# A mixture-of-experts layer: the experts' down product in three float32r passes, the routing weight folded into gate times up, g_ffn moved to the sums, and a scatter that skips empty places

## The chip, the cores and the metric

The program runs on one core of a Trainium2 chip. The metric is the device time of one execution in microseconds; the kernel before is given as the median of three runs.

## What is computed

Two transformer blocks run one after the other on 512 tokens of width 1024, in float32. The change lies in the mixture-of-experts part of the first block. Each token goes to 8 of 64 experts; its expert outputs are weighted, summed, multiplied by the row `g_ffn` and added to `x`.

```python
def swiglu(x, wg, wu, wd):
    return (jax.nn.silu(x @ wg) * (x @ wu)) @ wd
...
def moe_ffn(h, ...):
    scores = sigmoid(h @ w_router)
    _, idx = lax.top_k(scores + b_router, TOP_K)          # 8 of 64
    wts = (chosen scores / their sum * ROUTE_SCALE)
    ...
    def expert_block(acc, blk):                            # up to 128 rows of one expert
        tok, wt, e = blk
        yb = swiglu(h_pad[tok], w_e_gate[e], w_e_up[e], w_e_down[e]) * wt[:, None]
        return acc.at[tok].add(yb), None
    ...
    return swiglu(h, w_sh_gate, w_sh_up, w_sh_down) + routed[:n]
...
    y = moe_ffn(h2, ...)
    return x + g_ffn * y.reshape(b, s, d)
```

An expert's gate and up weights are 1024x256 each, its down weights 256x1024: 3 MB in all.

## The kernel before

The program goes through the first block's attention and gating (to about 600 us), the router, the experts (about 620 to 1358 us), a short turn to the second block (to about 1395 us), and the second block with its own large products. `moe` (L763) runs the experts.

**One expert** is `expert_block` (L1040). 128 places hold the expert's tokens; a place without a token is empty. The tokens' rows `xg` were gathered from DRAM (`expert_rows`, indices `gidx`). TensorE transposes them (`p_xt`, 8 transposes) and `split` (L104) cuts the result into a float32r high part (ScalarE, L105) and a low part (VectorE, L106): `xt`. The gate and up weights come as two 1 MB loads (`raw`), are split in four pieces of 128x1024 into `whi` and `wlo` (the pool `pair`, three buffers each), and each piece serves 6 products of `mm` (L91: high by high, high by low, low by high, all float32r): 24 matmuls of 512 columns into `p_gu`. ScalarE takes Silu of the gate half (L1060), VectorE multiplies by the up half (L1061): `ea`. Two transposes (`p_at`, L1064) and a copy by VectorE (L1066) make `eat`.

**The down product** is in plain float32 (L1072): four matmuls, from `eat` and the third `raw` buffer as it was loaded, into two banks `p_y`. In the profile each float32 matmul shows as two instructions. VectorE then reads each bank and multiplies by the place's routing weight `wsl` and by `grow`, which is `g_ffn` laid over all partitions (L1075): `ey`. A DMA issued by GpSimd scatters the 128 rows of `ey` and adds them in DRAM into `yd` (L1076). The two tensors `yd` have 640 rows: an empty place p has the index 512 + p, so its row is added into a spare row that nobody reads. The gather takes the same indices with a bound of 511, and skips them. Successive experts alternate between the two `yd`; the last two share one.

64 experts and one spare block (`spare`, L1088, for tokens beyond 128) make 65 such blocks; the loop `overflow` runs no further block here. Beside them run the shared expert's products (`p_sh`, L983 and L1011), the lists of places (`slots`), and transposes of `x`.

**What sets the order.** Over most of the experts' part a scheduler of the framework sets each engine's order at build time; each engine then works its list strictly in that order. Waits are semaphores. The loads go through SP's queue into nine `raw` buffers in turn: six of the pool `raw2` (`RAW2`, L31) and three of `raw`. The first six loads are issued during the product before (L668).

**The turn** to the second block: `routed_first` (L1135) loads the first `yd` (two tiles `raw`), `routed_second` (L1144) adds it to `x`; the second `yd` is loaded as four tiles `yx` (L1210) after the last scatter has landed, and `routed` adds each (L1217), multiplies by the norm's row (L1218) and sums squares, tile by tile. TensorE's next products (`p_xh`, L1237) wait for that.

## Time and profile before

| | |
|---|---|
| Runs of the kernel before (us) | 3177.44, 3180.88, 3176.13; median 3177.44 |
| The profiled execution (us) | 3173.92, its span 3172.1 |
| Experts' part, from its first `p_y` to its last | 635.8 to 1357.2 us |
| Engines over the whole span | TensorE 97% busy, VectorE 71%, ScalarE 44%, GpSimd 18% |
| DMA over the whole span | 251 GB/s mean |

An engine's busy share is an average over stages with different limits, so the experts' part is read by itself: how much of it each engine works, what ended each engine's waits, and what the DMA queues carried. "PE" is TensorE, "PEld" its weight loads, "DVE" VectorE, "ACT" ScalarE, "POOL" GpSimd, "SPq" the queue of loads.

### The profile page before, as it was taken

The numbers are of one execution on the slowest core, as the hardware profiler recorded it, in microseconds if no ns is written. First come the engines' busy times: TensorE is split into PE (matmuls) and PEld (weight loads), VectorE is DVE, ScalarE is ACT, GpSimd is POOL, SyncE is SP. The second block draws the span as 40 slices with busy tenths as digits, with TensorE's granted clock in tenths as the row PEclk, the third lists the DMA queues.
The fourth block names the chain that finished last, engine by engine and source line by source line (L and its number), as shares of the span: only waits on it lengthen the run. The fifth ranks groups of instructions, "written<-read, shape, count | busy, mean of one in ns | idle before, by whom it ended". The sixth has DMA issues, their size and how long they took to land.

```text
span 3172.1 us, 43671 instructions
## 1 busy us (share of the span) xinstructions
PE 3062.8 (97%) x16232; PEld 2479.5 (78%) x16232; DVE 2238.7 (71%) x4079; ACT 1383.4 (44%) x2199; POOL 578.9 (18%) x448
## 2 busy tenths in 40 slices
PE   8999999999999999969999999999999999999999
PEld 4777888666666766657777788899999998888887
DVE  7467654587777777756633334899998887888887
ACT  5257423454444544434445324544444443333332
POOL 0200000122222222200000000033333233222221
PEclk9999999899999999989999999999999999999999
DMA  7554545399999999952121122487789989999997
GB/s 248 175 159 145 220 158 203 125 359 338 335 344 334 358 349 346 317 170 83 41 85 62 70 93 95 139 283 268 278 312 348 332 332 344 349 348 354 353 339 270
DMA packets 237626, 782.01 MB, mean 247 GB/s; under 512 B 28884, under 2 KB 110292, under 8 KB 191588
## 3 DMA queue, kind: packets, MB, share of 16 engines
q1 hardware_dynamic: 169072, 574.02, 49.0%
q0 software_dynamic: 65424, 198.81, 20.2%
q10 hardware_dynamic: 2916, 6.37, 0.6%
q8 instruction: 128, 2.10, 0.3%
q14 instruction: 86, 0.70, 0.1%
HBM read 694.38 MB, written 101.97 MB: 251 GB/s over the span
## 4 chain that ended last, share of the span: by engine, by line
PE 49%; DVE 6%; issue 1%; ACT 1%; DMA 1%; ACTq 0%; DVEq 0%; POOL 0%; POOLq 0%
PE p_y L102 16%; PE p_pu L102 12%; PE p_za L102 3%; PE p_z L102 2%; PE p_all L1267 2%; PE p_rg L102 1%; DVE wlo L106 1%; PE p_pq L102 1%; PE p_mx L102 1%; PE p_yr L102 1%; DVE prow L2010 1%; PE r_s L1614 1%; PE r_y L1624 1%; PE p_ya L102 1%; PE p_gt L1979 1%
## 5 line engine op out<-in xcount | busy, mean ns | idle before, releaser
L105 ACT ACTIVATE whi<-raw 128x1024 fp32r<-128x1024 f32 (+1 forms) x686 | 711.5, 1049 | 1135.4 <-PE p_pu L102 259.7
L106 DVE TENSOR_TENSOR wlo<-raw,whi 128x1024 fp32r<-128x1024 f32 (+1 forms) x686 | 822.6, 1207 | 350.2 <-ACT whi L105 338.9
L102 PE MATMUL p_pu<-xp,whi 128*128 128x384 f32 x2048 | 531.3, 338 | 5.0 <-ACT pact L1845 4.8
L102 PEld LDWEIGHTS p_pu<-xp,whi 128*128 128x128 f32 x2048 | 369.2, 188 | 7.9 <-ACT pact L1845 7.6
L102 PE MATMUL p_gu<-whi,xt 128*128 128x512 f32 x1040 | 356.8, 411 | 0.2 <-ACT whi L105 0.2
L102 PE MATMUL p_pu<-xp,wlo 128*128 128x384 f32 x1024 | 344.8, 338 | 4.7 <-DVE wlo L106 4.7
L102 PE MATMUL p_y<-whi,vhi 128*128 128x512 f32 x768 | 299.1, 389 | 3.0 <-ACT vhi L2060 1.6
L102 PE MATMUL p_y<-wlo,vhi 128*128 128x512 f32 x768 | 298.9, 389 | 0.0
L2000 POOL DMA_INDIRECT prow<-in_pu_rows,rows x128 | 198.0, 1547 | 513.9 <-DVE prow L2010 365.6
L1072 PE MATMUL p_y<-raw,eat 128*128 128x512 f32 x520 | 237.1, 597 | 2.7 <-DVE eat L1066 1.5
L102 PE MATMUL p_y<-whi,vlo 128*128 128x512 f32 x768 | 237.8, 389 | 0.0
L102 PEld LDWEIGHTS p_gu<-whi,xt 128*128 128x128 f32 x1040 | 197.4, 190 | 50.4 <-issue 11.2
L102 PE MATMUL p_gu<-wlo,xt 128*128 128x512 f32 x520 | 223.0, 429 | 4.9 <-DVE wlo L106 4.7
L2000 POOL DMA_INDIRECT prow<-in_pv_rows,rows x128 | 139.5, 1090 | 363.0 <-DVE yr L2016 349.7
L102 PEld LDWEIGHTS p_pu<-xp,wlo 128*128 128x128 f32 x1024 | 192.3, 188 | 10.4 <-DVE wlo L106 10.2
L1072 PEld LDWEIGHTS p_y<-raw,eat 128*128 128x128 f32 x520 | 97.7, 191 | 101.6 <-issue 89.5
L102 PEld LDWEIGHTS p_y<-whi,vhi 128*128 128x128 f32 x768 | 144.1, 188 | 33.5 <-ACT vhi L2060 2.0
L1076 POOL DMA_INDIRECT yd<-ey,gidx x64 | 117.5, 1836 | 285.1 <-DVE ey L1075 268.1
L102 PEld LDWEIGHTS p_y<-wlo,vhi 128*128 128x128 f32 x768 | 144.2, 188 | 30.0
L102 PEld LDWEIGHTS p_y<-whi,vlo 128*128 128x128 f32 x768 | 144.2, 188 | 29.9
L2016 DVE SCALAR_TENSOR_TENSOR yr<-prow,pdots,yr 128x1024 f32<-128x1024 f32 x128 | 163.8, 1280 | 0.2
L2010 DVE SCALAR_TENSOR_TENSOR prow<-prow,xr 128x1024 f32<-128x1024 f32 x128 | 155.5, 1219 | 3.1 <-DMA prow<-in_pu_rows,rows 3.0
(703 smaller groups left out, 5558.7 us busy)
## 6 DMA issues: line engine op xcount, KB each, us to landing
raw<-in_w_moe SPq DMA_DIRECT2D x195, 1024.0 KB
raw<-in_pu SPq DMA_DIRECT2D x64, 1024.0 KB
raw<-in_pv_rows SPq DMA_DIRECT2D x64, 1024.0 KB
raw<-in_w_mod SPq DMA_DIRECT2D x24, 1024.0 KB
gd<-gst SPq DMA_DIRECT2D x12, 2048.0 KB
vgt<-gd SPq DMA_DIRECT2D x32, 768.0 KB
actd<-pact SPq DMA_DIRECT2D x54, 384.0 KB
vact<-actd SPq DMA_DIRECT2D x54, 384.0 KB
```

What stands on the lines that cost most here:

```text
L102: nc.tensor.matmul(out, a, b, start=start and i == 0, stop=stop and i == len(passes) - 1)
L105: self.nc.scalar.activation(hi, src, AF.Copy)
L106: (lo_engine or self.nc.vector).tensor_tensor(lo, src, hi.bitcast(F32), ALU.subtract)
L1072: nc.tensor.matmul(py, at[:, 128 * k:128 * k + 128], wd[:, 1024 * k + 512 * n:1024 * k + 512 * n + 512], start=k == 0, stop=k == 1)
L1076: nc.gpsimd.indirect_dma_start(out=yd[:], out_offset=bass.IndirectOffsetOnAxis(ap=gi, axis=0), in_=y[:], in_offset=None, bounds_check=639, ...
L1267: self.nc.tensor.matmul(pts[i][:, :264], w[a][:, 128 * k:128 * k + 128], self.hn[b][:, k, 264 * i:264 * i + 264], start=k == 0 and n == 0, ...
L1614: nc.tensor.matmul(pt[:m, :n], self.rk[r:r + 64, g, 128 * kt:128 * kt + m], self.rq[r:r + 64, g, 512 - n:], start=True, stop=True)
L1624: nc.tensor.matmul(o, sts[kt][:, 128 * (i - kt):128 * (i - kt) + 128], v[:, 128 * kt:128 * kt + 128], start=False, stop=kt == i)
L1979: nc.tensor.matmul(pt[:, i, :], hots["hot2"][:, g, :, t], hots["ghi"][:, g, :, t], start=True, stop=False)
L2000: nc.gpsimd.indirect_dma_start(out=t[:], out_offset=None, in_=A["pu_rows" if i < 128 else "pv_rows"], in_offset=bass.IndirectOffsetOnAxis( ...
L2010: nc.vector.scalar_tensor_tensor(t, t, 1.0, self.xr, ALU.mult, ALU.mult, accum_out=dots[:, k:k + 1])
L2016: nc.vector.scalar_tensor_tensor(self.yr, t, dots[:, k:k + 1], self.yr, ALU.mult, ALU.add)
```

## The change

1. The down product goes through `mm` in three float32r passes. `eat` becomes a high and a low tile (`split` of `p_at`), and the down weights are split in two pieces of 128x1024 into `dhi` and `dlo`, two buffers each, in the pool of the experts' small tiles. Both banks `p_y` are filled together, the first half of the weights for both and then the second.
2. The routing weight is multiplied in with gate times up (L1061). `ey` is then a plain copy out of `p_y`, by ScalarE.
3. `g_ffn` is multiplied into the sums, once for each of the two `yd` after they are loaded (in `routed_second` and in `routed`). `grow` moves to a pool that lives that long.
4. The scatter's bound is 511, so that it skips empty places, and `yd` has 512 rows.
5. `RAW2` is 4: seven `raw` buffers in turn, and the last two of the first six loads are issued by GpSimd, in `moe`, behind the first two gathers.

```diff
-RAW2 = 6
+RAW2 = 4
...
-            self.yd = [d.tile([640, 1024], F32, name=f"yd{i}") for i in range(2)]
+            self.yd = [d.tile([512, 1024], F32, name=f"yd{i}") for i in range(2)]
...
-                            for i in range(5):
+                            for i in range(4):
                                 nc.gpsimd.dma_start(y[128 * i:128 * i + 128, :], self.macc)
...
-        nc.vector.tensor_mul(a, a, pg[:, 256:])
+        nc.vector.scalar_tensor_tensor(a, a, ws, pg[:, 256:], ALU.mult, ALU.mult)
...
-        at = ms.tile([128, 256], F32, name="eat", tag="eat")
-        nc.vector.tensor_copy(at, pt[:, :256])
+        at = [ms.tile([128, 256], F32R, name=f"eat{i}", tag=f"eat{i}") for i in range(2)]
+        self.split(*at, pt[:, :256])
         y = ms.tile([128, 1024], F32, name="ey", tag="ey")
         wd = part(2)
+        py = [ps.tile([128, 512], F32, name="p_y", tag="y") for n in range(2)]
+        for k in range(2):
+            hi, lo = (ms.tile([128, 1024], F32R, name=n, tag=n) for n in ("dhi", "dlo"))
+            self.split(hi, lo, wd[:, 1024 * k:1024 * k + 1024])
+            for n in range(2):
+                self.mm(py[n], tuple(t[:, 128 * k:128 * k + 128] for t in at), (hi[:, 512 * n:512 * n + 512], lo[:, 512 * n:512 * n + 512]),
+                        k == 0, k == 1)
         for n in range(2):
-            py = ps.tile([128, 512], F32, name="p_y", tag="y")
-            for k in range(2):
-                nc.tensor.matmul(py, at[:, 128 * k:128 * k + 128], wd[:, 1024 * k + 512 * n:1024 * k + 512 * n + 512],
-                                 start=k == 0, stop=k == 1)
-            o = slice(512 * n, 512 * n + 512)
-            nc.vector.scalar_tensor_tensor(y[:, o], py, ws, self.grow[:, o], ALU.mult, ALU.mult)
+            nc.scalar.activation(y[:, 512 * n:512 * n + 512], py[n], AF.Copy)
         nc.gpsimd.indirect_dma_start(out=yd[:], out_offset=bass.IndirectOffsetOnAxis(ap=gi, axis=0),
-                                     in_=y[:], in_offset=None, bounds_check=639, oob_is_err=True, compute_op=ALU.add)
+                                     in_=y[:], in_offset=None, bounds_check=511, oob_is_err=False, compute_op=ALU.add)
...
         for x, y in zip(self.xr, self.y0):
+            self.nc.vector.tensor_mul(y, y, self.grow[:, None, :].to_broadcast([128, 2, 1024]))
             self.nc.vector.tensor_add(x, x, y)
...
+            nc.vector.tensor_mul(ys[t], ys[t], self.grow)
             nc.vector.tensor_add(x[t], x[t], ys[t])
```

The scheduler orders the experts' part anew. TensorE, about expert 30, before: transposes of a later expert's rows (`p_xt`), of this one's `ea` (`p_at`), products of the next expert (`p_gu`), and the down product in one piece.

```order
L1046 MATMUL p_xt<-ident,xg_5302 128x128 x8
L102 MATMUL p_gu<-whi,xt_9501 128x512
L1064 MATMUL p_at<-ident,ea 128x128 x2
L102 MATMUL p_gu<-wlo,xt_9501 128x512
L102 MATMUL p_gu<-whi,xt_9502 128x512
L102 MATMUL p_gu<-whi,xt_9501 128x512
L102 MATMUL p_gu<-wlo,xt_9501 128x512
L102 MATMUL p_gu<-whi,xt_9502 128x512
L102 MATMUL p_gu<-whi,xt_9501 128x512
L1072 MATMUL p_y<-raw,eat 128x512 x4
```

After, at a like place; of the two tiles `eat` the first (9041) is the high part and the second (9042) the low one.

```order
L102 MATMUL p_y<-dhi,eat_9041 128x512
L102 MATMUL p_y<-dlo,eat_9041 128x512
L102 MATMUL p_y<-dhi,eat_9041 128x512
L102 MATMUL p_y<-dlo,eat_9041 128x512
L102 MATMUL p_gu<-wlo,xt_9091 128x512
L102 MATMUL p_gu<-whi,xt_9092 128x512
L102 MATMUL p_gu<-whi,xt_9091 128x512
L102 MATMUL p_gu<-wlo,xt_9091 128x512
L102 MATMUL p_gu<-whi,xt_9092 128x512
L102 MATMUL p_gu<-whi,xt_9091 128x512
L102 MATMUL p_y<-dhi,eat_9042 128x512 x2
L102 MATMUL p_y<-dhi,eat_9041 128x512
```

The down product now stands in two parts with six products of another expert between them: the four matmuls that need only the high part of `eat` come first.

ScalarE, about the same experts, before: the splits of the weights and rows and Silu, the same sequence for each expert.

```order
L105 ACTIVATE whi<-raw 128x1024 x4
L105 ACTIVATE xt_7036<-p_xt 128x512 x2
L1060 ACTIVATE ea<-p_gu 128x256
L105 ACTIVATE whi<-raw 128x1024 x4
L105 ACTIVATE xt_7178<-p_xt 128x512 x2
L1060 ACTIVATE ea<-p_gu 128x256
```

After, for somewhat over two experts:

```order
L105 ACTIVATE dhi<-raw 128x1024 x2
L105 ACTIVATE eat_7991<-p_at 128x256
L1077 ACTIVATE ey<-p_y 128x512 x2
L105 ACTIVATE whi<-raw 128x1024 x3
L105 ACTIVATE dhi<-raw 128x1024 x2
L105 ACTIVATE whi<-raw 128x1024 x2
L1077 ACTIVATE ey<-p_y 128x512 x2
L105 ACTIVATE whi<-raw 128x1024
L105 ACTIVATE xt_8240<-p_xt 128x512 x2
L1060 ACTIVATE ea<-p_gu 128x256
L105 ACTIVATE whi<-raw 128x1024 x2
L105 ACTIVATE eat_8095<-p_at 128x256
```

Each expert has five more instructions on ScalarE, and the copies `ey`, which wait for the end of a down product, stand ahead of the next splits of weights.

VectorE in the turn, before: two tiles `yx` with what follows them.

```order
L1217 TENSOR_TENSOR h2f_4832<-h2f_4832,yx 128x1024
L1218 TENSOR_TENSOR x<-h2f_4832,gf 128x1024
L1221 TENSOR_SCALAR xst<-xst 128x1
L1217 TENSOR_TENSOR h2f_4832<-h2f_4832,yx 128x1024
L1218 TENSOR_TENSOR x<-h2f_4832,gf 128x1024
```

After:

```order
L1220 TENSOR_TENSOR yx<-yx,grow 128x1024
L1221 TENSOR_TENSOR h2f_4830<-h2f_4830,yx 128x1024
L1222 TENSOR_TENSOR x<-h2f_4830,gf 128x1024
L1225 TENSOR_SCALAR xst<-xst 128x1
L1220 TENSOR_TENSOR yx<-yx,grow 128x1024
L1221 TENSOR_TENSOR h2f_4830<-h2f_4830,yx 128x1024
L1222 TENSOR_TENSOR x<-h2f_4830,gf 128x1024
```

One multiplication stands ahead of each addition.

## Rows read from the trace of the kernel before

**Rows 1.** The page: each engine's busy time and share over the span.
```profile
PE 3062.8 (97%) x16232; PEld 2479.5 (78%) x16232; DVE 2238.7 (71%) x4079; ACT 1383.4 (44%) x2199; POOL 578.9 (18%) x448
```

**Rows 2.** Busy time by stretch: one slice of the experts' part, the whole part, three later stretches.
```profile
core 0: us, PE busy (x) PEld busy (x) DVE busy (x) ACT busy (x) POOL busy (x), PEclk, DMA share, GB/s
1100.00:1150.00 50.00, 47.72 (x200) 31.16 (x200) 36.07 (x57) 19.13 (x26) 12.46 (x9) 0.93 1.02 352
640.00:1357.00 717.00, 705.55 (x3020) 478.38 (x3019) 538.89 (x787) 345.20 (x461) 195.05 (x123) 0.99 0.98 339
2110.00:2300.00 190.00, 181.93 (x1017) 175.09 (x1017) 185.83 (x668) 86.86 (x123) 71.68 (x43) 1.00 0.77 274
2300.00:2400.00 100.00, 97.66 (x700) 92.95 (x699) 93.15 (x140) 44.21 (x73) 37.19 (x23) 1.00 0.89 324
2400.00:2600.00 200.00, 200.00 (x1483) 194.97 (x1482) 177.01 (x256) 88.92 (x145) 60.47 (x43) 1.00 0.91 335
```

**Rows 3.** Waits in the experts' part: waiter, what ended it, us, times, longest.
```profile
ACT whi L105 <- PE p_gu L102: 235.8, 113, 10.2
...
PE p_gu L102 <- DVE wlo L106: 4.7, 5, 1.6
```

**Rows 4.** Waits of SP's queue from 600 to 1400 us.
```profile
SPq L1027 <- DVE wlo L106: 318.4, 85, 15.7
SPq L1027 <- PE p_y L1072: 178.4, 51, 12.5
```

**Rows 5.** Timeline of TensorE: one down product and the next instruction; start, us, what.
```profile
1323.89 3.60 PE L1072 MATMUL p_y<-raw,eat 128*128 128x512 f32 x8
1327.33 0.60 PE L1046 MATMUL p_xt<-ident,xg 128*128 128x128 f32 x4
```

**Rows 6.** The chain in a later stage: 48 float32r matmuls of 512 columns in a row.
```profile
1812.59 11.14 PE p_za L102 x48
```

**Rows 7.** Groups of the experts' part by shape: count | busy, mean ns | idle before.
```profile
L106 DVE TENSOR_TENSOR wlo<-raw,whi 128x1024 fp32r<-128x1024 f32 x249 | 299.4, 1221 | 89.1 <-ACT whi L105 87.9
L105 ACT ACTIVATE whi<-raw 128x1024 fp32r<-128x1024 f32 x249 | 257.8, 1064 | 243.2 <-PE p_gu L102 235.8 <-PE p_at L1064 4.1 <-DVE ea L1061 0.9
...
L1075 DVE SCALAR_TENSOR_TENSOR ey<-p_y,wsl,grow 128x512 f32<-128x512 f32 x125 | 89.1, 745 | 12.4 <-PE p_y L1072 12.1
...
L105 ACT ACTIVATE xt<-p_xt 128x512 fp32r<-128x512 f32 x123 | 67.7, 595 | 72.6 <-PE p_gu L102 65.8 <-PE p_xt L1046 5.4
...
L1060 ACT ACTIVATE ea<-p_gu 128x256 f32<-128x256 f32 x63 | 24.6, 390 | 25.9 <-PE p_gu L102 25.9
```

**Rows 8.** DMA queues and indirect issues from 700 to 1300 us.
```profile
q1 hardware_dynamic: 23470, 165.89, 69.1%
q0 software_dynamic: 14813, 40.39, 29.7%
...
xg<-h2d,gidx POOLq DMA_INDIRECT x51
yd<-ey,gidx POOLq DMA_INDIRECT x50
```

**Rows 9.** The chain through the turn: start, us, what.
```profile
1354.00 1.54 DMA yd<-ey,gidx
...
1363.76 10.65 DMA yd<-ey,gidx
```

**Rows 10.** Timeline of the turn: start, us, engine, line, what.
```profile
1363.23 2.29 DVE L1146 TENSOR_TENSOR h2f<-h2f,raw 128x2048 f32<-128x2048 f32 x1 [4.63 <-DMA raw<-yd]
...
1379.10 1.22 DVE L1217 TENSOR_TENSOR h2f<-h2f,yx 128x1024 f32<-128x1024 f32 x1
...
1380.35 1.23 DVE L1218 TENSOR_TENSOR x<-h2f,gf 128x1024 f32<-128x1024 f32 x1
```

**Rows 11.** Timeline of the start: the first gather on GpSimd and two splits.
```profile
613.71 1.11 POOL L1031 DMA_INDIRECT xg<-h2d,gidx  x1 [14.09 <-DVE ov_t L1119]
...
629.92 2.00 ACT L105 ACTIVATE whi<-raw 128x1024 fp32r<-128x1024 f32 x2
```

More of the change, by code (lines that the diff above doesn't have):

```diff
@@ L716, in ffn_begin @@
         self.r4 = r.tile([128, 4], F32, name="r4")
+        self.grow = r.tile([128, 1024], F32, name="grow")
         r = self.pool(self.rs, "h2r", side="right")
@@ L771, in moe @@
             self.sact = q.tile([128, 2, 512], F32, name="sact")
-            self.grow = q.tile([128, 1024], F32, name="grow")
             self.xr = [t.rearrange("p a b -> p (a b)").rearrange("p (t d) -> p t d", d=1024) for t in self.h2f]
```

## The prediction

> **What bounds the kernel now.** I read the busy times by stretch first, then who waits for whom in the experts' part, then the sizes of single instructions there. Over the span TensorE is busy 97% [rows 1], but that is a mean over stages. In the experts' part, 640 to 1357 us, it is busy 705.55 of 717 us, at 0.99 of its clock, while VectorE has 538.89 (75%) and ScalarE 345.20 (48%); the DMA share is 0.98 [rows 2]. Two readings compete: TensorE or the transfers. The waits decide for TensorE: ScalarE waits 235.8 us for `p_gu` to give split buffers back, so it stands ahead of TensorE, and TensorE's largest wait for a split is 4.7 us [rows 3]. SP's queue waits for buffers to come free (318.4 and 178.4 us) [rows 4]; no compute engine has a load among its long waits. So the transfers keep up, with little to spare, and the time of this part is TensorE's work plus what it stands idle: 11.5 us, 1.6%. There are 65 expert blocks, and the window of 717 us holds 717 / 11.27 = 63.6 of them (721.4 us from the first `p_y` to the last, 64 steps).
>
> **TensorE's part of the change.** Before, the down product is 8 instructions: from 1323.89 to the next at 1327.33, 3.44 us, 0.430 each [rows 5]. A float32r matmul of 512 columns takes 11.14 / 48 = 0.232 us in a row of 48 [rows 6]. After, there are 2 halves x 2 banks x 3 passes = 12 of them: 2.79 us. That is 0.65 us less in each block, 65 x 0.65 = **-42 us**. All of it is on the path as long as TensorE is the bound.
>
> The Trainium skill, "FP8 and Floating Point Precision", section "TensorE Precision Notes", says that true FP32 takes four passes through the array, of which the change would drop one: 4 x 0.232 x 65 = 60 us by that rule, an estimate. The trace differs: it shows two instructions of 0.430 for a float32 matmul, 0.86 and not 4 x 0.232 = 0.93, and the measured one is used.
>
> **VectorE.** Each block gains two `dlo` of the shape of `wlo`, 299.4 / 249 = 1.20 us, and loses two `ey`, 89.1 / 125 = 0.71 [rows 7]: +0.98. The low part of `eat` takes the place of a copy of its size, and gate times up stays one instruction: 0. Over 63.6 blocks 538.89 + 62 = 601 us, now in 717 - 41 = 676 us: 89%.
>
> **ScalarE.** Each block gains two `dhi` like `whi`, 257.8 / 249 = 1.04, two `ey` out of a bank like `xt`, 67.7 / 123 = 0.55, and the high part of `eat`, about one Silu, 24.6 / 63 = 0.39 [rows 7]: +3.55. 345 + 226 = 571 of 676 us: 85%.
>
> **What the fuller engines cost TensorE.** Each works its list in order, so a matmul can now wait for a split that stands behind something else; before, this hardly occurred. No row of this part shows it; three later stretches do, where TensorE also lives on splits [rows 2]: VectorE at 88.5% leaves TensorE idle 0 of 200 us, at 93% 2.3%, at 98% 4.2%. With 89%, VectorE would be next to the first of them. But ScalarE is at 44 to 46% there and at 85% here, and its new copies `ey` wait for the end of a down product ahead of the next weights; the low `eat` needs ScalarE and then VectorE, one hand-over more than now. So I take the worst of the three, 4.2% of 676 = 28 us instead of 11.5: **+17 us**. Ends: 0, and twice that idle share (57 us, +45). Own buffers for `dhi` and `dlo` keep the splits of the down weights from taking the three pairs that feed `p_gu`; without them this term would be the main one.
>
> **The transfers.** 128 rows of 4 KB are 0.524 MB a scatter; 50 of them are 26.2 of the 40.39 MB of the software queue, and the 51 gathers have 14.2, 0.28 MB or some 68 rows each [rows 8]. So a gather, with a bound of 511, does leave out empty places, and the scatter will. 512 tokens x 8 fill 4096 of 65 x 128 = 8320 places; 65 rows less in each block. The queue holds the 16 engines 29.7% of 600 us for some 51 blocks, 3.5 us a block for about 196 rows; by rows that frees 1.2 us, more if an adding row costs more than a plain one. TensorE's new pace is 11.27 - 0.65 = 10.6 us and the transfers need 11.27 x 0.98 - 1.2 = 9.9 (93%): they stay hidden, for 0. If rows were not skipped, 11.0 us of transfers would be the new pace and eat the gain; that is a rival below. Two `raw` buffers less leave seven, over two blocks ahead of TensorE; and a down buffer is free after its split and not after its matmuls. 0, at most one late load of 3 us now and then, which is in the upper end.
>
> **The start.** The two loads that GpSimd now issues stand behind the first gathers, at 613.71 and just after [rows 11], and hold its next gathers back by their issue only. A load of 1 MB takes 3 us at the part's 339 GB/s [rows 2]; their data, expert 1's second half and down weights, are wanted near 630, when the splits of that time run [rows 11]. 0; if late, 3 to 4 us.
>
> **The turn.** Four multiplications of 128x1024 stand ahead of four additions of 1.22 us on VectorE, which works there almost without a gap (1379.10 to 1380.35 and on) [rows 10]: 4 x 1.22 = **+4.9 us**. The two in `routed_second` take 2 x 2.29, from 1363.23 to 1372.4 with the additions, under the last scatter, which lands at 1374.4 [rows 9, 10]: 0 (4.6 if that cover were gone). The last two scatters stand one behind the other (1354.00 to 1363.76, then 10.65 us) [rows 9], each with half its rows: 2 x 1.2 = **-2.4 us**. Together +2.5. The two DMAs less that zero `yd` lie far ahead of any use: 0.
>
> **Sum.** -42 + 17 + 2.5 = -22.5 on the profiled execution's 3173.9: 3151.4. The median of the runs stands 3.5 us above that execution, so 3155 against 3177.4. By the ends of the waits this case goes from 3138 (none added) to 3172 (idle share near 7%).
>
> **Rivals.**
> 1. *The transfers were a bound too.* For: their share of 0.98. Against: the loads wait for buffers and not engines for loads. Then the freed 1.2 us a block also takes away TensorE's idle 11.5 us and the stretch at lower clock (0.93 over 1100 to 1150 [rows 2], 3.5 us): 3177.4 - 42 - 15 + 2.5 = 3123.
> 2. *VectorE sets the pace*, as its 89% and the order allow: `dlo` and the low `eat` come behind `wlo` for the next block, so that TensorE idles some 8%: 54 us instead of 11.5, which eats the 42: 3180, the same within the measurement. The Trainium skill, "Perfetto Trace Analysis", section "Identifying the Most-Contended Engine", would have TensorE judged by the busy share of its weight loads, 478 of 717 us or 67%, against VectorE's 75%; by that, VectorE is already the fuller one and this rival the forecast. The trace does not agree so far: the waits run the other way.
> 3. *The scatter skips nothing*, so the change doesn't do what it says: the transfers hold the pace at 11.0 to 11.3 us, 3165 to 3180. The gathers' bytes speak against it.
> 4. *Slower: waits that drop the clock.* Where TensorE waits for a split between the two parts of a down product, its clock can fall to half. Row 1100 to 1150 shows one such spell: 2.3 us idle and a mean of 0.93 of the clock, 3.5 us lost, near 5 us in all. The gain of 40 us is gone at 8 more spells; with one in every fourth block (16), 3177.4 - 40 + 80 = 3217. For: five hand-overs a block instead of three, and three of four resources near 90%. Against: the first four matmuls need only the high part, and other products stand between.
>
> **Chances.** The forecast 0.58, rival 1 0.13, rivals 2 and 3 0.17, rival 4 0.12. A measurement of this kernel can tell about 0.2%, 6.4 us, from no change. Faster by more than that (under 3171) are the forecast's all but the last of its range, rival 1 and a little of rival 3: 0.72. Within it 0.16, slower 0.12. The range leaves out rival 4 and the far end of rival 1: 3123 to 3180. The forecast's own is 3138 to 3172.
>
> **What would show it.** Twelve `p_y` of 0.232 us a block, and blocks 10.6 to 10.9 us apart; VectorE 87 to 90% and ScalarE 82 to 86% in the part; TensorE's idle 20 to 40 us, with `dlo`, `eat` or `wlo` as its releasers; the software queue's bytes down by 17 MB; four more multiplications in the turn and `p_xh` some 2 us later after the last block. It is wrong if TensorE's waits for VectorE come to 50 us or more, if its clock in the part is under 0.97, or if splits wait for loads.

## The result and the profile after

The changed kernel takes **3197.80 us** (median of 4 runs, 3194.58 to 3201.98) against 3177.89 for the kernel before (3176.13 to 3180.88). The ratio is 1.0066, with a 95% interval of 1.0054 to 1.0079: 20 us slower. The forecast was 3155, 22 us faster, and its range ended at 3180. Both are wrong, the sign too.

The profiled execution took 3198.96 us (span 3197.2), 25 us more than the one of before. By marks in the two traces: the first `p_gu` came at 626.2 instead of 620.1; from the first block's `p_at` to the last one's, 64 steps, it took 738.8 us instead of 720.4; the turn from the last `p_y` to the last `p_xh` took 37.2 instead of 37.0; what lies behind that took 1776 instead of 1778. So 18 of the 25 us lie in the experts' part, although its matmuls got shorter, and 6 in a later start.

From the page: busy time, share and instructions of each engine (before in [rows 1]).

```profile
PE 3043.0 (95%) x16492; PEld 2528.2 (79%) x16492; DVE 2312.1 (72%) x4085; ACT 1585.6 (50%) x2524; POOL 599.9 (19%) x448
```

The software queue over 700 to 1300 us: packets, MB, share of the 16 engines (before in [rows 8]).

```profile
q0 software_dynamic: 14665, 26.87, 18.7%
```

The scatter does skip its empty places: 26.87 MB and 18.7% of the 16 engines where [rows 8] has 40.39 MB and 29.7%. The experts' part as one stretch, 640 us to its end (busy time of PE, weight loads, DVE, ACT, POOL; granted clock, DMA share, GB/s; before in [rows 2]):

```profile
640.00:1384.00 744.00, 693.76 (x3313) 532.70 (x3311) 611.91 (x797) 547.68 (x789) 217.58 (x125) 0.98 0.89 311
```

TensorE stands idle 744 - 693.8 = 50 us of this stretch; before it was 11.5. VectorE is at 82%, ScalarE at 74%, the transfers at 0.89: nothing is full. The stall is a matter of who hands what to whom, and when. The longest waits of TensorE's weight loads for another engine in the same stretch (us in total, times, longest):

```profile
PEld p_gu L102 <- DVE wlo L106: 24.3, 33, 1.5
PEld p_gu L102 <- ACT whi L105: 14.7, 17, 2.8
PEld p_y L102 <- ACT eat L105: 14.1, 12, 2.2
PEld p_xt L1046 <- DVE xt L106: 11.2, 9, 2.6
```

And those of ScalarE:

```profile
ACT xt L105 <- PE p_gu L102: 77.6, 41, 4.9
ACT dhi L105 <- PE p_y L102: 44.2, 30, 7.9
ACT whi L105 <- PE p_gu L102: 36.9, 42, 3.1
```

In [rows 3] ScalarE waited 235.8 us for `p_gu` to give split buffers back: it stood ahead. Now that wait is 36.9, and TensorE waits for four kinds of split. The timeline of one such place (start, us, engine, line, operation, count; the wait before it in brackets):

```profile
1270.10 0.40 PE L102 MATMUL p_y<-dhi,eat 128*128 128x512 f32 x1
...
1270.33 0.39 PE L102 MATMUL p_y<-dlo,eat 128*128 128x512 f32 x1
...
1270.56 0.40 PE L102 MATMUL p_y<-dhi,eat 128*128 128x512 f32 x1
...
1272.65 1.07 ACT L1077 ACTIVATE ey<-p_y 128x512 f32<-128x512 f32 x2
...
1273.61 1.05 ACT L105 ACTIVATE dhi<-raw 128x1024 fp32r<-128x1024 f32 x1
...
1273.74 0.38 PE L1064 MATMUL p_at<-ident,ea 128*128 128x128 f32 x2
...
1274.55 2.00 ACT L105 ACTIVATE whi<-raw 128x1024 fp32r<-128x1024 f32 x2
...
1275.66 0.50 PE L102 MATMUL p_gu<-whi,xt 128*128 128x512 f32 x1 [1.53 <-ACT whi L105]
...
1276.45 0.38 ACT L105 ACTIVATE eat<-p_at 128x256 fp32r<-128x256 f32 x1
...
1276.88 0.57 PE L102 MATMUL p_y<-dhi,eat 128*128 128x512 f32 x1 [0.72 <-ACT eat L105]
...
1277.25 0.63 PE L102 MATMUL p_y<-dlo,eat 128*128 128x512 f32 x1
1277.67 0.63 PE L102 MATMUL p_y<-dhi,eat 128*128 128x512 f32 x1
```

The `p_y` come 0.23 us apart at first, as forecast. But ScalarE's list has `ey`, `dhi` and two `whi` ahead of the `eat` that TensorE needs, so the transposes end at 1274.1 and the down product starts at 1276.88. Then the `p_y` come 0.42 apart. The windows of that stretch show the granted clock (0.57, so mostly the lower of its two levels, 1.2 GHz), right behind the idle spell:

```profile
1277.00:1281.00 4.00, 4.00 (x11) 3.14 (x12) 2.71 (x4) 0.94 (x2) 0.00 (x0) 0.57 1.04 287
```

There are seven such spells of 3.4 us in the part, 24 us in all, where the kernel before had two of 6.8, 14 us in all.

### The profile page after: what moved, and what is told of

It is laid out like the page before. It is cut to its first block, busy times and chain, and to the rows that moved or that the text cites. A ratio compares the mean times of both kernels' runs of the same rounds, so it can differ in the third digit from the quotient of the medians.

```text
span 3197.2 us, 44642 instructions
## 1 busy us (share of the span) xinstructions
PE 3043.0 (95%) x16492; PEld 2528.2 (79%) x16492; DVE 2312.1 (72%) x4085; ACT 1585.6 (50%) x2524; POOL 599.9 (19%) x448
## 4 chain that ended last, share of the span: by engine, by line
PE 75%; DVE 10%; ACT 5%; issue 5%; DMA 5%; POOL 0%; SPq 0%; ACTq 0%; DVEq 0%; POOLq 0%
PE p_y L102 19%; PE p_pu L102 11%; PE p_gu L102 8%; DVE wlo L106 3%; PE p_za L102 3%; PE p_ga L102 3%; PE p_z L102 2%; ACT whi L105 2%; PE p_in L102 2%; PE p_all L1271 1%; PE p_rg L102 1%; PE p_pq L102 1%; PE p_mx L102 1%; PE p_out L102 1%; PE p_ua L102 1%
## 5 line engine op out<-in xcount | busy, mean ns | idle before, releaser
L102 PE MATMUL p_gu<-whi,xt 128*128 128x512 f32 x1040 | 350.2, 406 | 11.4 <-ACT whi L105 9.8
L102 PEld LDWEIGHTS p_gu<-whi,xt 128*128 128x128 f32 x1040 | 199.3, 192 | 59.9 <-ACT whi L105 14.7
L102 PE MATMUL p_y<-dhi,eat 128*128 128x512 f32 x520 | 180.3, 408 | 13.7 <-ACT eat L105 10.8
L106 DVE TENSOR_TENSOR dlo<-raw,dhi 128x1024 fp32r<-128x1024 f32 x130 | 157.9, 1221 | 40.1 <-ACT dhi L105 39.1
L102 PEld LDWEIGHTS p_y<-whi,vhi 128*128 128x128 f32 x768 | 144.2, 188 | 33.5 <-ACT vhi L2064 2.0
L105 ACT ACTIVATE dhi<-raw 128x1024 fp32r<-128x1024 f32 x130 | 137.5, 1066 | 44.7 <-PE p_y L102 44.2
```

What stands on the lines that cost most here:

```text
L102: nc.tensor.matmul(out, a, b, start=start and i == 0, stop=stop and i == len(passes) - 1)
L105: self.nc.scalar.activation(hi, src, AF.Copy)
L106: (lo_engine or self.nc.vector).tensor_tensor(lo, src, hi.bitcast(F32), ALU.subtract)
```

## What the runs told apart

Two theories stood at the start. **A**: ScalarE's list, filled by `dhi`, `eat` and `ey`, starves TensorE of splits. **R**: it is something else in the change. The texts set apart below were written before each run; other letters in them name further theories, V that VectorE's load is what counts and B that the fewer weight buffers are. Differences below are medians against runs of the kernel before that were taken beside them.

**Halves of the change.** First everything but the three passes:

```diff
-        at = [ms.tile([128, 256], F32R, name=f"eat{i}", tag=f"eat{i}") for i in range(2)]
-        self.split(*at, pt[:, :256])
+        at = ms.tile([128, 256], F32, name="eat", tag="eat")
+        nc.vector.tensor_copy(at, pt[:, :256])
...
-            self.split(hi, lo, wd[:, 1024 * k:1024 * k + 1024])
...
+                nc.tensor.matmul(py, at[:, 128 * k:128 * k + 128], wd[:, 1024 * k + 512 * n:1024 * k + 512 * n + 512],
+                                 start=k == 0, stop=k == 1)
```

> The changed kernel with its down product put back into float32 (eight matmuls on the unsplit weights, no dhi, dlo and split eat); the rest of the change stays: weight in gate times up, g_ffn on the sums, scatter with a bound of 511, four early weight buffers, ey copied by ScalarE. Theory A (ScalarE's list, filled by dhi, eat and ey in strict order, starves TensorE of splits): without the splits of the down product the 20 us of the experts' part go away; what stays is the turn (+1 to +3 us) and the start (+2 to +3): 3176 to 3184 us, blocks 11.27 us apart, TensorE idle under 20 us in the part. Rival R (it is the rest of the change, fewer early buffers, copies by ScalarE or the scatter, that costs): 3195 or more.

Measured: 3200.45 us, +24.8 (ratio 1.0078, 1.0062 to 1.0095). Then the other half, the diff's `eat`, `dhi`, `dlo` and three passes on the kernel before, with `RAW2 = 4` for the room and this line kept:

```diff
+            nc.vector.scalar_tensor_tensor(y[:, o], py[n], ws, self.grow[:, o], ALU.mult, ALU.mult)
```

> The kernel before with the three float32r passes alone (dhi, dlo, split eat, and the four early weight buffers that make room for them); the weight and g_ffn stay on VectorE where ey leaves the bank, and the scatter keeps its 640 rows. VectorE then has its 539 us plus 2 x 1.20 x 63.6 = 153, some 692 us. Theory A: ScalarE has two copies less in each block than in the changed kernel, so fewer of its hold-ups, but VectorE has two more, and the part can't be shorter than some 700 us by VectorE alone: 3185 to 3215. Rival V (VectorE's load is what counts): VectorE is full, the part is over 760 us, 3215 or more. Rival R: under 3178, since the rest that costs is gone.

Measured: 3201.46, +25.8 (1.0059 to 1.0093). Each half costs what the whole costs, so the costs don't add. Theory A's range held for the second run but not for the first, and it can hardly be the answer there: that kernel has neither `dhi` nor a split `eat`, only the copies `ey`. What the halves share is `RAW2 = 4`.

**Where the copies and splits run.** In the changed kernel `ey` moved from ScalarE to VectorE, and in another `dlo` from VectorE to GpSimd:

```diff
-            nc.scalar.activation(y[:, 512 * n:512 * n + 512], py[n], AF.Copy)
+            nc.vector.tensor_copy(y[:, 512 * n:512 * n + 512], py[n])
...
-            self.split(hi, lo, wd[:, 1024 * k:1024 * k + 1024])
+            self.split(hi, lo, wd[:, 1024 * k:1024 * k + 1024], nc.gpsimd)
```

> The changed kernel with ey copied out of its bank by VectorE instead of ScalarE. Theory A: ScalarE no longer stands at ey for the end of the down product ahead of the next whi; its two copies of 0.60 us a block go, so TensorE's waits for whi and eat (39 us of the queues' waits) fall to under 15 while those for wlo and xt rise with VectorE at 92 to 95%: 3180 to 3195. Rival V (VectorE's load is what costs): 128 more copies of some 0.65 us on VectorE make it worse by 20 to 60 us, 3215 to 3260.

> The changed kernel with dlo made by GpSimd instead of VectorE. Rival V: VectorE loses 124 x 1.22 = 151 us of work in the part, its waits go, 3150 to 3165. Theory A: ScalarE's list is the same, so TensorE's waits for whi and eat stay; only those for wlo and xt fall: 3180 to 3200; a dlo by GpSimd that takes over 3 us or holds back gathers and scatters adds to that, 3200 to 3230.

Measured: 3204.49, +28.8 (1.0076 to 1.0109), and 3343.68, +168. Every range was missed: the first came out between theory A's and rival V's, the second above both. With `ey` on VectorE the experts' part reads:

```profile
640.00:1380.00 740.00, 690.66 (x3269) 526.10 (x3267) 671.82 (x917) 488.50 (x651) 245.45 (x123) 0.98 0.90 310
```

VectorE has 60 us more work than in the changed kernel (611.91) and ScalarE 59 less (547.68), and the time differs by 9 us. So neither VectorE's load, against the second rival, nor `ey` on ScalarE decides by itself. The GpSimd run shows its price in the groups by shape (count, busy us, mean ns, idle before):

```profile
L106 POOL TENSOR_TENSOR dlo<-raw,dhi 128x1024 fp32r<-128x1024 f32 x130 | 343.2, 2664 | 192.6 <-ACT dhi L105 192.0
```

A `dlo` takes GpSimd 2.66 us, VectorE 1.22, and GpSimd waits 192 us at it for `dhi` with its gathers and scatters queued behind. At that price the run doesn't tell theory A from rival V.

**The parts alone.** Four buffers, the scatter, and the moves, each on the kernel before; and the moves with `ey` on VectorE and all the rest but the three passes:

```diff
-RAW2 = 6
+RAW2 = 4
```

```diff
-            self.yd = [d.tile([640, 1024], F32, name=f"yd{i}") for i in range(2)]
+            self.yd = [d.tile([512, 1024], F32, name=f"yd{i}") for i in range(2)]
...
-                                     in_=y[:], in_offset=None, bounds_check=639, oob_is_err=True, compute_op=ALU.add)
+                                     in_=y[:], in_offset=None, bounds_check=511, oob_is_err=False, compute_op=ALU.add)
```

```diff
-        nc.vector.tensor_mul(a, a, pg[:, 256:])
+        nc.vector.scalar_tensor_tensor(a, a, ws, pg[:, 256:], ALU.mult, ALU.mult)
...
-            nc.vector.scalar_tensor_tensor(y[:, o], py, ws, self.grow[:, o], ALU.mult, ALU.mult)
+            nc.scalar.activation(y[:, 512 * n:512 * n + 512], py, AF.Copy)
...
+            self.nc.vector.tensor_mul(y, y, self.grow[:, None, :].to_broadcast([128, 2, 1024]))
...
+            nc.vector.tensor_mul(ys[t], ys[t], self.grow)
```

The fourth is the first run of this section with this line:

```diff
-            nc.scalar.activation(y[:, 512 * n:512 * n + 512], py, AF.Copy)
+            nc.vector.tensor_copy(y[:, 512 * n:512 * n + 512], py)
```

> The kernel before with four early weight buffers in place of six, and nothing else. The two runs that split the change, everything but the three passes and the three passes alone, were each 25 us slower than before; this is one of the two things that they share. Theory B (fewer weight buffers: expert loads start later, the split weights stand less far ahead of TensorE, and the planned order of the splits changes): 3190 to 3205, with TensorE's waits for xt and wlo as in those two runs. Theory A (ScalarE's list, filled by the splits and copies that the change adds): no such work is added here, 3175 to 3180.

> The kernel before with the scatter alone changed: 512 rows, a bound of 511, empty places left out. The transfers fall by 16 MB on the software queue, TensorE is the bound: theory A and theory B both expect 3170 to 3178, 0 to 7 us faster. If the planned order of the engines' lists, which moves with every edit, is itself worth some 20 us (theory O), this run too is 10 us or more off from before, without any work added.

> The kernel before with the weight in gate times up, ey copied by ScalarE and g_ffn on the sums; six early weight buffers, float32 down product and 640 rows as before. Theory A: ScalarE waits at ey for the end of the float32 down product (110 us of waits, 85 times, in the run of everything but the three passes) ahead of xt and whi, so this is as slow as that run: 3190 to 3205. Theory B: the buffers are all there, only the turn's 3 to 5 us are added: 3176 to 3184.

> As the run of everything but the three passes (four early weight buffers, scatter with a bound of 511, weight in gate times up, g_ffn on the sums, float32 down product), with ey copied by VectorE as before instead of ScalarE. Theory A: back to before plus the turn: 3176 to 3184. Theory B: as slow as that run, 3192 to 3205.

Measured: four buffers 3191.90, +13.8 (1.0031 to 1.0065); the scatter 3176.86, -1.3 (0.9992 to 1.0011); the moves with six buffers 3174.15, -4.0 (0.998 to 0.9999); the last 3203.01, +24.9 (1.0069 to 1.0102). Theory B, the buffers, was right in three (in the scatter's run it said the same as A) and 2 us off in the fourth. `ey` on ScalarE costs nothing where the buffers are six.

**Late loads or a shorter ring?** `RAW2 = 4` does two things: two loads of expert 1 are issued later, by GpSimd, and the ring of weight buffers has seven places instead of nine. Here only the first:

```diff
-                if m < RAW2:
+                if m < 4:
...
-            for m in range(RAW2, 6):
+            for m in range(4, 6):
```

> The kernel before with its six early weight buffers, nine in the ring, but with two of the six early loads issued later, by GpSimd behind the first gathers, as the change does. Four buffers alone cost 14 us. Theory B1 (what counts is how far the ring of buffers reaches: nine weight loads ahead of their use against seven): nothing changes here, 3175 to 3182. Theory B2 (what counts is that two loads start late): as with four buffers, 3188 to 3195.

Measured: **3166.38, -11.9** (ratio 0.9959, 0.9947 to 0.9972), better than both kernels, which neither theory had foreseen. So the ring alone costs 13.8 + 11.9 = 26 us. The two kernels differ in nothing but its size. With nine places, the longest wait of TensorE's weight loads for another engine in the part, and then ScalarE's two:

```profile
PEld p_gu L102 <- DVE wlo L106: 4.0, 7, 1.7
```

```profile
ACT whi L105 <- PE p_gu L102: 235.3, 131, 9.4
ACT xt L105 <- PE p_gu L102: 65.6, 40, 9.9
```

With seven places, the same two views:

```profile
PEld p_xt L1046 <- DVE xt L106: 11.3, 7, 1.6
PEld p_y L1072 <- DVE eat L1066: 9.0, 13, 1.2
PEld p_gu L102 <- DVE wlo L106: 7.7, 13, 1.2
```

```profile
ACT whi L105 <- PE p_gu L102: 216.3, 106, 12.4
ACT xt L105 <- PE p_gu L102: 121.7, 43, 6.8
ACT whi L105 <- DMA raw<-in_w_moe: 16.7, 7, 5.6
```

With seven places some splits do wait for a load (16.7 us), but TensorE's long waits are for `xt` and `eat`. The instruction lists differ too: the scheduler plans another order. ScalarE's list, with nine places (-) and seven (+):

```
 L105 ACTIVATE xt_6371<-p_xt 128x512 x2
 L1060 ACTIVATE ea<-p_gu 128x256
-L105 ACTIVATE whi<-raw 128x1024 x4
+L105 ACTIVATE whi<-raw 128x1024 x6
 L105 ACTIVATE xt_6478<-p_xt 128x512 x2
 L1060 ACTIVATE ea<-p_gu 128x256
-L105 ACTIVATE whi<-raw 128x1024 x4
+L105 ACTIVATE whi<-raw 128x1024 x2
 L105 ACTIVATE xt_6576<-p_xt 128x512 x2
```

Four splits between two `xt` become six and two in turn. Counted in the traces from 640 to 1345 us, six in a row stand 14 to 17 times in the changed kernel, in the run of four buffers alone and in the two without the three passes, 6 times in the three passes alone and 7 in the changed kernel with `ey` on VectorE (all seven places), and 3 to 5 times in the kernels with nine and without the passes. Behind six, `xt` comes later for the transposes that need its bank. In the run without the three passes only one split waits for a load (2.6 us), and its ring costs as much (28 us, below); so there it is hardly late data, which leaves the order. The count of sixes alone is not its measure, since the kernels with 6 and 7 of them are as slow. How much of the 26 us is which can't be told, since the ring sets both.

**A whole ring with three passes.** `dhi` and `dlo` take 16 KB of each partition, as much as two ring places. To have both, room has to come from elsewhere. First from a single `ey` and two `xg`:

```diff
-        y = ms.tile([128, 1024], F32, name="ey", tag="ey")
+        y = ms.tile([128, 1024], F32, name="ey", tag="ey", bufs=1)
...
-            self.xg = [q.tile([128, 1024], F32, name=f"xg{i}") for i in range(3)]
+            self.xg = [q.tile([128, 1024], F32, name=f"xg{i}") for i in range(2)]
```

With them went `RAW2 = 6` and three each of `dhi` and `dlo` by 512 columns (and one `shy`, the shared expert's copy); `RAW2 = 5` and full tiles; and, as a control, the kernel before with the first's small buffers and nothing else:

```diff
+                hi, lo = (ms.tile([128, 512], F32R, name=t, tag=t, bufs=3) for t in ("dhi", "dlo"))
+                self.split(hi, lo, wd[:, 1024 * k + 512 * n:1024 * k + 512 * n + 512])
```

> The changed kernel with six early weight buffers again. The room comes from dhi and dlo in tiles of 512 columns, three each, from one ey in place of two, two xg in place of three and one buffer for the copies of the shared expert. Theory B1 (the ring of buffers is what the change lost): the 19 us that four buffers cost in the experts' part come back, and some of the gain forecast from the three passes stays: 3155 to 3178. Theory A (the added splits and copies hold up TensorE by themselves): 3185 or more.

> The changed kernel with five early weight buffers, dhi and dlo as in the change; the room comes from one ey in place of two and two xg in place of three. Theory B1: between the change's 3198 and the run with six: 3175 to 3190. Theory A: 3190 to 3205, since every added split is there.

> The kernel before with the room given up that the two runs with more buffers take: one ey, two xg, one buffer for the copies of the shared expert. GpSimd's gathers wait for their buffer long before they are needed, so both theories expect 3175 to 3185. If this is 3190 or more, one ey or two xg cost by themselves, and the runs with five and six buffers carry that cost too.

Measured: 3260.99 (+82.7), 3244.98 (+66.7), 3261.27 (+83.0). Theory A's 3185 or more held for the first, the other ranges were missed. But the control, put at 3175 to 3185, is as slow, so these say little on the passes. Its reason stands among VectorE's waits:

```profile
DVE ey L1075 <- DMA yd<-ey,gidx: 87.3, 30, 8.2
```

A single `ey` waits until the scatter has read it. Now with two `ey` again, two `xg` and one `shy`, and two loads issued late as above: `RAW2 = 6` with halves (`bufs=2`), `RAW2 = 5` with full tiles, and a control; and beside them the first run of this section with `RAW2 = 6`, late issue and all three `xg`:

> The changed kernel with six early weight buffers, nine in the ring (four loaded early and two by GpSimd, as in the change), and two ey as in the change. The room comes from dhi and dlo in tiles of 512 columns, two each, two xg in place of three and one buffer for the copies of the shared expert. It differs from the control of this call by the three passes, the moves and the scatter. Theory B1 (the seven-buffer ring is what the change lost; three passes gain when the ring is whole): 3130 to 3165, under the control. Theory A (the added splits hold up TensorE whatever the ring): the gain of 42 us in TensorE's work is eaten again, 3165 to 3195, level with the control or above it.

> The changed kernel with five early weight buffers, eight in the ring (four loaded early), dhi and dlo and ey as in the change; the room comes from two xg in place of three and one buffer for the copies of the shared expert. Theory B1: 3165 to 3185, half of the way from 3198 to the run with six. Theory A: 3190 to 3200, as the change.

> The kernel before with two of the six early loads issued later by GpSimd, as in the run of 3166 us, and with two xg in place of three and one buffer for the copies of the shared expert: the control of this call. If two xg cost nothing it stands at 3163 to 3172; the waits for gathers were 3 to 5 us in the two runs with two xg, so up to 3180 is open.

> The changed kernel without its three passes and with its six early weight buffers, two of them loaded later by GpSimd: float32 down product, weight in gate times up, ey by ScalarE, g_ffn on the sums, scatter with a bound of 511. Theory B1: the moves alone were -3, the scatter alone -1, the later issue alone -12: 3158 to 3172. Theory A, by which ey on ScalarE costs: 3180 or more.

Measured: 3205.76 (+29.2), 3202.90 (+26.4), the control 3213.15 (+36.6), and all of the change but the three passes on nine places 3173.35 (-3.2; 0.9984 to 1.0004). Two `xg`, with the single `shy`, cost 36.6 + 11.9 = 48 us. The two kernels with the passes came out above both theories' ranges, and the control above its own; only the last, 1 us over theory B1's, tells B1 from A. It is the change without its passes and without the short ring: level with before, 28 us better than the same with seven places. Last, with three `xg` and nine places, once with halves (`bufs=2`) and single small buffers, once without own buffers for `dhi` and `dlo`:

```diff
+        a = ms.tile([128, 256], F32, name="ea", tag="ea", bufs=1)
...
+        at = [ms.tile([128, 256], F32R, name=f"eat{i}", tag=f"eat{i}", bufs=1) for i in range(2)]
```

```diff
-            hi, lo = (ms.tile([128, 1024], F32R, name=n, tag=n) for n in ("dhi", "dlo"))
+            hi, lo = (self.pair.tile([128, 1024], F32R, name="d" + n, tag="w" + n) for n in ("hi", "lo"))
```

> The changed kernel with nine weight buffers in the ring (four loaded early, two by GpSimd), three xg and two ey as in the change. The room comes from dhi and dlo in tiles of 512 columns, two each, and from single buffers for ea, the split eat, the hot masks and the copies of the shared expert. It differs from the kernel of 3173 us (all of the change but the three passes, with nine in the ring) by the three passes and these single buffers. Theory B1 (three passes gain once the ring is whole): 3135 to 3165. Theory A (the added splits hold up TensorE whatever the ring): 3175 to 3200, so 0 to 25 above that kernel although TensorE's matmuls are 42 us shorter, with waits for dhi, dlo, eat, whi and wlo of 60 us or more.

> The changed kernel with nine weight buffers in the ring, three xg and two ey, where dhi and dlo have no buffers of their own: they take turns with whi and wlo in the three pairs, and the shared expert's copies have one buffer. Each block then sends six splits through the three pairs instead of four. Theory B1: the ring is whole, but the pairs are the next bound: 3150 to 3185. Theory A: ScalarE's list is as full as in the change and the splits stand less far ahead: 3190 to 3230.

Measured: 3215.34 (+37.1; 1.0099 to 1.0143) and 3301.96 (+123.7), both above every range. The waits of TensorE's weight loads, of the former, then of the latter:

```profile
PEld p_y L102 <- DVE dlo L106: 23.7, 52, 1.2
PEld p_gu L102 <- DVE wlo L106: 13.6, 21, 1.1
PEld p_y L102 <- ACT dhi L105: 11.3, 18, 1.4
PEld p_y L102 <- ACT eat L105: 10.2, 13, 1.4
```

```profile
PEld p_xt L1046 <- DVE xt L106: 98.5, 51, 2.1
PEld p_gu L102 <- DVE wlo L106: 48.6, 102, 2.8
PEld p_gu L102 <- ACT whi L105: 31.3, 53, 2.6
```

So the step of the prediction that own buffers spare the pairs holds: without them it is 104 us worse than the change, though on nine places. And the passes gain nothing that can be told from the noise in any arrangement that was run:

| three passes added to | change of the median |
|---|---|
| seven places, `ey` on ScalarE (the change) | 24.8 to 19.9: -5 us |
| seven places, `ey` on VectorE | 24.9 to 28.8: +4 us |
| seven places, nothing else of the change | 13.8 to 25.8: +12 us |
| nine places, two `xg`, with the moves and scatter | 36.6 to 29.2: -7 us |
| nine places, single `ea` and `eat`, halved `dhi` and `dlo` | -3.2 to 37.1: +40 us |

The first three rows differ by the passes alone. In the fourth the moves and the scatter come in too, and in the last the small buffers and the halves, whose own cost no run shows. Each run's interval is 3 to 7 us to either side, so a difference of two carries some 7 us: -5, +4 and -7 can't be told from nothing, and +12 only just. Nine places with full `dhi` and `dlo` and all else as in the change do not fit beside the other tiles, so that was not run, and what the passes do there stays open.

## Why the prediction was wrong, point by point

The same 64 steps, from the first block's `p_at` to the last one's, in the columns of [rows 2], for six kernels. Before and after the change:

```profile
632.30:1352.90 720.60, 710.11 (x3042) 482.00 (x3040) 544.76 (x794) 349.63 (x468) 195.23 (x123) 0.99 0.98 340
640.20:1379.10 738.90, 689.99 (x3299) 530.42 (x3298) 607.57 (x793) 546.86 (x787) 217.38 (x125) 0.98 0.89 311
```

Everything but the three passes, on seven places; then four buffers alone, seven places:

```profile
633.40:1377.10 743.70, 716.96 (x3042) 481.50 (x3040) 469.76 (x668) 418.74 (x596) 184.47 (x124) 0.99 0.90 313
632.80:1372.00 739.20, 713.24 (x3041) 479.75 (x3040) 550.03 (x795) 348.62 (x468) 195.71 (x124) 1.00 0.99 336
```

Everything but the three passes, on nine places; then two loads issued later, nine places:

```profile
634.60:1349.00 714.40, 706.52 (x3041) 479.87 (x3040) 470.87 (x668) 415.45 (x595) 190.94 (x123) 1.00 0.91 320
634.80:1349.30 714.50, 707.04 (x3041) 480.81 (x3040) 546.17 (x794) 351.82 (x468) 199.46 (x123) 1.00 0.99 343
```

Over these steps TensorE is busy 20 us less after than before, where 42 were forecast, and idle 48.9 us instead of 10.5.

- **The bound.** TensorE was the bound before, as read. The scatter alone took the software queue from 40.39 MB [rows 8] to 27.28 over the same 600 us and left the time as it was (-1.3 us), so the transfers were not, and the first rival falls:

```profile
q0 software_dynamic: 14841, 27.28, 18.8%
```

  The Trainium skill's rule in "Perfetto Trace Analysis", section "Identifying the Most-Contended Engine", would have put VectorE ahead of TensorE in the changed kernel too (611.9 against 532.7 us of weight loads); 60 us of work moved from ScalarE to VectorE cost 9 us, so the trace doesn't bear that out. Neither engine was full; what broke was the lead of the splits.
- **"Two `raw` buffers less leave seven, over two blocks ahead of TensorE", priced at 0: the step that failed first.** It looked for late loads only, and put one late load now and then into the upper end. It cost 26 us at equal issue, and 28 between the two kernels with everything but the passes. TensorE's idle time is 743.7 - 717.0 = 26.7 and 739.2 - 713.2 = 26.0 with seven places and 7.9 and 7.5 with nine. The ring's size is an input of the scheduler, so it moved the order, as ScalarE's list shows, and that had no term.
- **-42 us of matmuls, all of it on the path: right in pace, too large in effect, the second step that failed.** Where TensorE is fed, twelve `p_y` stand 0.23 us apart, in place of eight at 0.43. But from the kernel without the passes to the changed one, both on seven places, TensorE's busy time falls by 27 us only (716.96 to 689.99). Of the other 15, some 5 are the lower clock (24 us of spells against 14 before; the granted clock is 0.98, without the passes 0.99 as before). Most of the rest may stand behind waits: the `p_gu` behind the wait at 1275.66 shows 0.50 us where one in a row follows the last after 0.23, and in the 64 steps TensorE's matmuls wait 63 times against 33 without the passes, 30 x 0.27 = 8 us, an estimate.
- **+17 for the fuller engines, ends 0 and +45: near in size, from a ground that the runs don't bear out.** The passes add 22 us of idle time (26.7 to 48.9). So they came to -27 + 22 = -5 us, where -42 + 17 = -25 was forecast; the other 16 us of new idle time are there without them. The load of both engines was forecast well (612 and 548 us, forecast 601 and 571). But the waits were priced by the busy share of VectorE, from stretches where ScalarE was half idle, and with VectorE at 91% and ScalarE at 66% the time moved by 9 us. The trace points to the lists instead: `dhi` waits 44.2 us for `p_y`, with the `whi` and `eat` that TensorE needs next behind it. No run changes that alone, so it is not shown. The upper end was also summed wrongly: -42 + 45 + 2.5 gives 3183, and the forecast's range was ended at 3172.
- **The start: wrong both ways.** The two loads issued by GpSimd were put at 0, or 3 to 4 us if late. In the changed kernel the first `p_gu` came 6.1 us later. With nine places, this later issue alone gains 11.9: the two profiled executions are 7.4 us apart (3164.7 against 3172.1), of which the part is 6 us shorter (714.4 for 64 steps), the turn 3.5 shorter (33.5), and the first `p_gu` 2.5 later (622.6); the rest is that the profiled execution of before lies below its median. The waits of TensorE's weight loads for `wlo` are 4.0 us there instead of 7.6. Why the later issue makes the part and the turn shorter is open.
- **The second rival, VectorE sets the pace,** put TensorE's idle time at 54 us, near the 50 measured, but VectorE is at 82%, and the waits are for both engines: 24.3 and 11.2 us for `wlo` and `xt`, 14.7 and 14.1 for ScalarE's `whi` and `eat`.
- **The fourth rival, waits that drop the clock,** named a loss that is there and put it too high. There are five spells more than before, and together 10 us more at half the clock, some 5 us lost. The larger part of the loss is plain idle time.
- **The signs of being wrong** that the prediction named did not come: the waits of weight loads for VectorE are 45 us in all (50 was the sign), the clock is 0.98, and no split waits for a load. Of the marks that it named for being right, these were missed: idle time of 20 to 40 us (50), blocks 10.6 to 10.9 us apart (11.5), VectorE at 87 to 90% (82%) and ScalarE at 82 to 86% (74%).
- **The transfers and the scatter: right.** 18.7% of 600 us in place of 29.7% for 50 blocks is 1.3 us a block (forecast 1.2), hidden, and alone worth nothing that can be measured (0.9992 to 1.0011).
- **The turn: right within some 2 us** (0.3 us longer, forecast 2.5). The four multiplications take 1.22 us each, and the halved last scatter 8.29 us where [rows 9] has 10.65:

```profile
1386.55 8.29 DMA yd<-ey,gidx
```

That was the chain of waits; VectorE's timeline behind it:

```profile
1399.16 1.22 DVE L1220 TENSOR_TENSOR yx<-yx,grow 128x1024 f32<-128x1024 f32 x1
1400.41 1.22 DVE L1221 TENSOR_TENSOR h2f<-h2f,yx 128x1024 f32<-128x1024 f32 x1
```

The sum that the runs give: -12 (later issue), +26 (ring of seven), +11 (moves and scatter on that ring, 24.8 - 13.8), -5 (three passes, within the noise) = +20. Each term is the difference of two runs in a row, so they add up by themselves. The parts are not independent: the scatter, the moves and the later issue alone are -1, -4 and -12, together -3; beside the later issue the moves and the scatter cost 9 us on nine places (-3.2 + 11.9) and 11 on seven, and why is open. The later issue, which leaves the engines' work as it was, moved this kernel by 12 us, and no count of that work shows it.

## What to carry to other kernels

A buffer that feeds a scheduler's plan was not free here: price a smaller ring by changing it alone, before adding the edit that needs its room. Where an engine lives on splits made by others, ask how far ahead of it they stand and what waits in front of them in the same list; busy shares of 82% and 74% did not show it here. And taking work from the bound engine pays only as long as those who feed it can keep their lead: here 42 us of shorter matmuls came to 27 us less busy time, and 22 us more idle time.

## What was not expected of the hardware

A subtraction of 128x1024 takes GpSimd 2.66 us and VectorE 1.22. A scatter holds its source long: with one `ey`, VectorE waited 87 us in 30 blocks for it, up to 8.2 us each. And the scatter with a bound of 511, changed alone, moved 13.1 MB less in 600 us and freed 11% of the 16 DMA engines, without a change in time that can be measured.
